# The four taps of the short convolution: accumulated in PSUM in two halves of 512 tokens, or in SBUF over all 1024

## The chip, the cores and the metric

The kernel runs on one core of a Trainium2 chip. The metric is the device time of one execution in microseconds (us), as the median of several runs. A profiled execution of the kernel gives the trace that the rows below are read from. The engines are named as the profile names them: PE is the tensor engine (PEld its weight loads), DVE the vector engine, ACT the scalar engine, POOL the GpSimd engine, and SP the engine that issues the DMAs. Each engine works through its own instructions strictly in the order in which they stand.

## What is computed

One layer of a hybrid decoder block on 1024 tokens with 1024 channels. A layer norm is followed by one input projection, whose columns go to two branches: a Mamba-2 (SSD) branch and a conformer convolution branch. Cut to what matters here:

```python
h = layer_norm(x, ln_emb_g, ln_emb_b)
proj = einsum('bld,de->ble', h, w_in)
xs, z, bm, cm, dt_raw, glu, cgate = split(proj)

xbc = concat([xs, bm, cm])                       # 1536 channels
xbc = silu(causal_depthwise_conv(xbc, ssm_conv_w, ssm_conv_b))   # 4 taps
...                                              # chunked scan, gate by silu(z), norm

u = glu[..., :1024] * sigmoid(glu[..., 1024:])
u = causal_depthwise_conv(u, conf_conv_w, conf_conv_b)           # 31 taps
u = silu(layer_norm(u)) * silu(cgate)
...
out = concat([y_ssm, u]) @ w_out + b_out         # then norm, per-layer gate, norm
```

The change is in the convolution with four taps, over the 1536 channels of `xbc`.

## The kernel before

Channels lie on the 128 partitions and tokens along the free dimension, so a tile is 128 channels by 1024 tokens, all in 32 bits. The input projection makes 44 such column tiles. For each one, `weights` loads the raw weights, ACT rounds them (`wh`, L119) and POOL takes the rest (`wl`, L120); `inproj` then runs 24 matmuls of 512 columns for each half of the tokens into one PSUM bank `ps` (L123 to L125), and ACT copies the bank out. There are three such banks, used in turn, so PE can run at most three halves ahead of ACT.

The tiles come in a fixed order. In each of eight rounds `conf_tile` makes the two tiles of a gated unit (`ga` L262, `tb` L265, multiplied into `u` at L279) and a convolution of 31 taps: six of the eight on DVE, which accumulates in a PSUM pair `pc` of 1024 columns (L291), and two (rounds 1 and 5) as products on ACT (`prod`, L285) that POOL adds up (`acc`, L286). Two other tiles follow in each round. Twelve of those are `xbc_tile`, the place of the change: ACT copies both halves into `xin` (L373), ACT makes the first tap (`cacc`, L247), DVE adds three more (L377), ACT applies the Silu (L378), and a DMA stores the tile. Others are `dt_path` (small DVE operations, L336 to L351), `decays`, and `z_tile` (L383). After the last round come `cs` (a sum on POOL, L630), `conf_norm` (its first matmul is `mu`, L390), the first `prep` (its transposes are `xtok`, L461, into the same PSUM pair as `pc`), and then the scan by chunks, the output projection and the gates.

A scheduler orders the instructions of each engine from its own estimates of time; the code sets what depends on what. PSUM has eight banks, all given out: three to `ps`, two to a tag `o` that serves small jobs in turn, one to a tag `b`, and two to the pair.

Of the kernel before, what the change touches and what calls it, by code (L numbers as in the profile page):

```python
# [11 lines left out]
ALU = mybir.AluOpType  # L12
# [13 lines left out]

# columns of the per-channel vectors
VEC = {}
# [18 lines left out]
def tile_block(ctx: ExitStack, tc: tile.TileContext, x, pT, wple, win, wdt, wout, wgate, vec, rows, heads, out):  # L47
# [17 lines left out]

# [1 line left out]
    BUFS = {"gt": 4, "xd": 2, "u": 2, "ha": 3, "y": 2, "xb": 2, "st": 1}  # L67
# [19 lines left out]

# [1 line left out]
    vc = const.tile([P, NVEC], F32, name="vc")  # L89
# [13 lines left out]
    nc.gpsimd.memset(mhalf, -0.5)  # L103
    # [s, l]: 1 where l >= s
    tri = const.tile([P, P], F32, name="tri")
    nc.gpsimd.affine_select(out=tri, in_=ones, pattern=[[1, P]], compare_op=ALU.is_ge, fill=0.0, base=0, channel_multiplier=-1)
    # adds rows h, 16 + h and 32 + h
    fold = const.tile([P, HEADS], F32, name="fold")
# [8 lines left out]
    def split(src, h, l, leng):  # L117
        """h: src rounded to the tensor engine's 12 bits; l: what is left, exactly."""
        nc.scalar.copy(out=h.bitcast(F32R), in_=src)  # L119
        leng.tensor_tensor(out=l.bitcast(F32R), in0=src, in1=h, op=ALU.subtract)  # L120
# [16 lines left out]
    def moments(src, tag):  # L137
        """mean and rstd of the rows of src [P, 1024]."""
        st = wk.tile([P, 2, 6], F32, name="st" + tag, tag="st" + tag)
        for i in range(2):  # L140
            nc.vector.bn_stats(out=st[:, i, :], in_=src[:, i * 512:(i + 1) * 512])
        mv = small("mv" + tag, 2)
        nc.vector.bn_aggr(out=mv, in_=st)
        return mv[:, 0:1], rstd_of(mv[:, 1:2], 1, tag, nc.gpsimd)
# [6 lines left out]

# [1 line left out]
    xts = [regB.tile([P, D], F32, name="xt", tag="B1") for t in range(NT)]  # L153
# [26 lines left out]

# [1 line left out]
    def weights(ct):  # L182
# [17 lines left out]
    def residual():  # L200
        ag, abb, bob = (work(n, "ha") for n in ("ag", "abb", "bob"))
        for i, tl in enumerate((ag, abb, bob)):
            nc.sync.dma_start(out=tl, in_=rows[i:i + 1, :].broadcast_to([P, D]))
        nc.gpsimd.tensor_scalar(out=ag, in0=ag, scalar1=ALPHA, scalar2=0.0, op0=ALU.mult, op1=ALU.add)
        nc.gpsimd.tensor_scalar(out=abb, in0=abb, scalar1=ALPHA, scalar2=0.0, op0=ALU.mult, op1=ALU.add)
        nc.gpsimd.tensor_tensor(out=abb, in0=abb, in1=bob, op=ALU.add)
        # alpha * h + b_out, by tokens
        for t in range(NT):
            nc.gpsimd.tensor_tensor(out=xts[t], in0=xts[t], in1=ag, op=ALU.mult)
            nc.gpsimd.tensor_tensor(out=xts[t], in0=xts[t], in1=abb, op=ALU.add)  # L210
            nc.sync.dma_start(out=ha_d[t], in_=xts[t])

    def ple_all():
        """the projected per-layer input, by tokens."""
        parts = {}
        tags = iter(["u", "u", "xd", "xd", "gt", "gt", "ha", "ha"])
        for src, nm in ((wple, "wp"), (pT, "pp")):
            for k in range(2):
                raw = work(nm + "raw", "xb") if nm == "wp" else regB.tile([P, L], F32, name=nm + "raw", tag="B2")
                parts[nm, k] = (raw, work(nm + "H", next(tags)), work(nm + "L", next(tags)))  # L220
        for half in range(2):
            hs = slice(half * 512, half * 512 + 512)
            for k in range(2):
                for src, nm in ((wple, "wp"), (pT, "pp")):
                    nc.sync.dma_start(out=parts[nm, k][0][:, hs], in_=src[:, k, hs])
                    split(*(a[:, hs] for a in parts[nm, k]), nc.vector)
        embed_load(0)
        nc.sync.dma_start(out=vc, in_=vec)
        nc.vector.tensor_scalar(out=hb, in0=v("bglu", 0, 16), scalar1=0.5, scalar2=None, op0=ALU.mult)
        parts = {i: (a[1].bitcast(F32R), a[2].bitcast(F32R)) for i, a in parts.items()}  # L230
        for t in range(NT):
            tk = slice(t * P, (t + 1) * P)
            pl = work("pl", "xb" if t % 4 > 1 else "y", L)
            for n in range(2):
                nn = slice(n * 512, n * 512 + 512)
                ps = bank("psp")
                for k in range(2):
                    three(ps, parts["pp", k][0][:, tk], parts["pp", k][1][:, tk], parts["wp", k][0][:, nn], parts["wp", k][1][:, nn], k == 0, k == 1)
                if (t + n) % 2:
                    nc.vector.tensor_copy(out=pl[:, nn], in_=ps)  # L240
                else:
                    nc.scalar.copy(out=pl[:, nn], in_=ps)
            nc.sync.dma_start(out=ple_d[t], in_=pl)
# [10 lines left out]
    def conf_tile(j):  # L254
        """GLU and the causal convolution of 128 channels."""
        ga = work("ga", "gt")
# [44 lines left out]
    def dt_path():  # L301
# [7 lines left out]
        nc.sync.dma_start(out=hd, in_=heads.unsqueeze(0).broadcast_to([P, 2, HEADS]))  # L309
        # both parts of the weights side by side  # L310
        nc.scalar.copy(out=wh2[:, :, 0:HEADS].bitcast(F32R), in_=raw)
# [22 lines left out]

        # softplus(v) = max(v, 0) + 2 atanh(e / (2 + e)), e = exp(-|v|)
        nc.vector.tensor_tensor(out=b3(vv), in0=b3(pst[:, 0:P]), in1=bh(hd[:, 0, :]), op=ALU.add)  # L336
# [16 lines left out]
    def decays():  # L353
        """dec holds dt * a at first: its sums over the tokens of each chunk, and what follows from them."""
        ar, er = (wk.tile([P, P], F32, name=n, tag="dg") for n in ("ar", "er"))
# [14 lines left out]
    def xbc_tile(ct, i):  # L370
        xin = work("xin", "xb", 3 + L)
        nc.gpsimd.memset(xin[:, 0:3], 0.0)
        inproj(ct, lambda hs, ps: nc.scalar.copy(out=xin[:, 3 + hs.start:3 + hs.stop], in_=ps))  # L373
        acc = work("cacc", "ha")
        first_tap(FT4, acc, xin[:, 0:L], v("scw", i * 4), v("scb", i))
        for j in range(1, 4):
            nc.vector.scalar_tensor_tensor(out=acc, in0=xin[:, j:j + L], scalar=v("scw", i * 4 + j), in1=acc, op0=ALU.mult, op1=ALU.add)  # L377
        nc.scalar.activation(out=acc, in_=acc, func=AF.Silu)  # L378
        nc.sync.dma_start(out=xbc_d[:, :, i, :].rearrange("t p l -> p t l"), in_=by_chunk(acc))
# [36 lines left out]
    def out_weight(src, get, tag, last, scale=None, leng=nc.gpsimd):  # L416
        """last: a place for the raw one, where those that share the tag leave none."""
        raw = work("wor", last) if last else get("wor", tag)
# [8 lines left out]

# [1 line left out]
    state = work("state", "st")  # L429
# [8 lines left out]
    def prep(c):  # L438
        """what chunk c needs besides the state: decays times C.B, x * dt, B by tokens."""
        xb = slabs(work("xb", "xb", 12 * P), 12)  # L440
# [8 lines left out]
        for q in range(2):  # L449
            er = ea_d[c * HEADS:(c + 1) * HEADS, :].rearrange("(t q) l -> q t l", q=2)[q]  # L450
            nc.sync.dma_start(out=ea[q * HD:(q + 1) * HD], in_=er.unsqueeze(0).broadcast_to([HD, NK, P]))
        # exp(acs[l] - acs[s]); the part l < s is held at exp(0) here and dropped with C.B
        for h in range(HEADS):
# [30 lines left out]
    def chunk(c, sz, xb, gg, ea, xdt, xdd, btok):  # L484
        y = slabs(work("y", "y"))
        for g in range(2):
            # from the state, scaled by exp(acs[l])
            ys = y[:, g * 4:g * 4 + 4, :]
# [34 lines left out]
    def mean_square(c, y, ea):  # L523
        """rstd of the two groups of channels of the gated output."""
        sq = ea.rearrange("p (g t) l -> p g t l", g=2)
# [21 lines left out]
    def conf_out(c, mH, mL, ha):  # L547
        """conformer half of the output projection"""
        for n in range(2):
# [14 lines left out]
    def affine(o, src, mu, rs, g, b):  # L564
        """(src - mu) * rs * g + b"""
        nc.vector.scalar_tensor_tensor(out=o, in0=src, scalar=mu, in1=g, op0=ALU.subtract, op1=ALU.mult)
        nc.vector.scalar_tensor_tensor(out=o, in0=o, scalar=rs, in1=b, op0=ALU.mult, op1=ALU.add)

    def out_proj(c, yH, yL):
        """the SSM half of the output projection, and the norm"""  # L570
        r = work("r", "ha")
# [21 lines left out]
    def gate(c, r, hTH, hTL):  # L593
        """the per-layer input, gated, and the norm"""
        pl = work("pl3", "st")
# [75 lines left out]

# [1 line left out]
    ready, last = out_proj(0, *ys.pop(0)), None  # L673
# [58 lines left out]
```

## Time and profile before

| What | Value |
|---|---|
| Time, median of 3 runs | 932.74 us (928.87 to 934.99) |
| Span of the profiled execution | 927.1 us |
| PE busy | 877.1 us, 95% of the span |
| DVE busy | 708.6 us, 76% |
| POOL busy | 534.4 us, 58% |
| ACT busy | 364.8 us, 39% |
| Mean granted clock of PE | 0.985 of full speed |

The span runs from the first to the last instruction of the profiled execution; the timed runs stand 1.8 to 7.9 us above it. Busy shares are means over stages with different limits, so they say little about any one stage.

### The profile page before, as it was taken

To read this page: it belongs to the slowest core of one execution; us is meant where nothing else is said; L and a number is where in the kernel's file an instruction comes from. 1 tells how busy PE (TensorE), PEld (TensorE's weight loads), DVE (VectorE), ACT (ScalarE), POOL (GpSimd) and SP (SyncE) were. 2 spreads that over 40 slices of the span, in tenths; PEclk is the share of its full clock that TensorE was granted. 3 is DMA by queue.
4 is the path that set the end of the run, shared out by engine and by line. 5 is a ranking of instruction groups with operands and counts; after the bars stand their busy time and mean duration, and the time that the engine had idled before them with its cause. 6 is when DMAs were issued, how large, how long until landed. Compare 5 with 4: busy or idle time off the path is not lost.

```text
span 927.1 us, 10959 instructions
## 1 busy us (share of the span) xinstructions
PE 877.1 (95%) x4141; PEld 711.0 (77%) x4141; DVE 708.6 (76%) x830; ACT 364.8 (39%) x513; POOL 534.4 (58%) x298
## 2 busy tenths in 40 slices
PE   6989998989999999999899999999999889999996
PEld 5857787868787888788688887777777668888885
DVE  7868997498999989989626523998885786666665
ACT  3532244665423435555446533644343421111001
POOL 2559836999924249999792254676757442222211
PEclk9999999989999999999999999999999999999999
DMA  9703241321213121322322388888887902222111
GB/s 337 264 24 107 77 157 46 96 69 46 78 37 113 52 86 53 123 97 80 114 100 83 103 304 271 300 273 230 283 264 261 353 25 92 91 90 91 69 46 68
DMA packets 67716, 126.42 MB, mean 136 GB/s; under 512 B 4176, under 2 KB 41552, under 8 KB 67664
## 3 DMA queue, kind: packets, MB, share of 16 engines
q1 hardware_dynamic: 67664, 125.73, 40.4%
q8 instruction: 32, 0.52, 0.2%
q14 instruction: 20, 0.16, 0.1%
HBM read 89.93 MB, written 35.78 MB: 136 GB/s over the span
## 4 chain that ended last, share of the span: by engine, by line
PE 47%; DVE 20%; POOL 13%; DMA 11%; issue 6%; ACT 3%; SPq 1%; POOLq 0%; DVEq 0%; ACTq 0%
POOL acc L286 8%; DVE pc L291 7%; PE ps L123 6%; PE ps L124 6%; PE ps L125 6%; DVE cacc L377 4%; PE psg L123 3%; PE psg L125 3%; PE psg L124 3%; DMA wor<-in_wout_dram 3%; PE pss L123 3%; PE pss L125 3%; PE pss L124 3%; DMA xb<-xbc_d 2%; POOL wl L120 2%
## 5 line engine op out<-in xcount | busy, mean ns | idle before, releaser
L123 PE MATMUL ps<-hH,wl 128*128 128x512 f32 x704 | 278.4, 397 | 12.7 <-ACT ga L262 6.2
L124 PE MATMUL ps<-hL,wh 128*128 128x512 f32 x704 | 278.0, 395 | 1.0 <-DVE hL L179 1.0
L125 PE MATMUL ps<-hH,wh 128*128 128x512 f32 x704 | 278.1, 395 | 0.0
L291 DVE SCALAR_TENSOR_TENSOR pc<-u,vc,pc 128x1024 f32<-128x1024 f32 x174 | 223.8, 1286 | 4.5
L123 PEld LDWEIGHTS ps<-hH,wl 128*128 128x128 f32 x704 | 133.9, 191 | 44.7 <-issue 7.7
L286 POOL TENSOR_TENSOR acc<-acc,prod 128x1024 f32<-128x1024 f32 x60 | 160.2, 2671 | 13.3 <-ACT acc L282 9.3
L124 PEld LDWEIGHTS ps<-hL,wh 128*128 128x128 f32 x704 | 134.2, 191 | 29.3 <-DVE hL L179 1.5
L125 PEld LDWEIGHTS ps<-hH,wh 128*128 128x128 f32 x704 | 134.2, 191 | 28.4 <-issue 0.2
L120 POOL TENSOR_TENSOR wl<-wraw,wh 128x1024 fp32r<-128x1024 f32 x44 | 110.6, 2513 | 53.2 <-ACT wh L119 23.0
L132 POOL TENSOR_SCALAR ve<-mv 128x1 f32<-128x1 f32 x24 | 21.7, 907 | 121.3 <-DVE mv L611 88.4
L285 ACT ACTIVATE prod<-u,vc 128x1024 f32<-128x1024 f32 x60 | 68.8, 1150 | 51.4 <-POOL acc L286 44.9
L377 DVE SCALAR_TENSOR_TENSOR cacc<-xin,vc,cacc 128x1024 f32<-128x1024 f32 x36 | 76.9, 2135 | 7.4 <-ACT cacc L247 4.7
L119 ACT CAST wh<-wraw 128x1024 fp32r<-128x1024 f32 x44 | 46.2, 1051 | 82.6 <-DMA wraw<-in_win_dram 47.8
L455 DVE TENSOR_SCALAR gt<-gt,acs 128x128 f32<-128x128 f32 x128 | 42.0, 397 | 25.4 <-POOL qs L398 17.3
L123 PE MATMUL psg<-woh,hTL 128*128 128x512 f32 (+1 forms) x136 | 52.9, 389 | 4.8 <-DVE hTL L120 4.8
L123 PE MATMUL pso<-woh,mL 128*128 128x512 f32 x128 | 51.6, 406 | 2.8 <-POOL mL L120 1.8
L123 PE MATMUL pss<-woh,yL 128*128 128x512 f32 x128 | 50.8, 397 | 3.4 <-DVE r L580 3.4
L120 POOL TENSOR_TENSOR wol<-wor,woh 128x1024 fp32r<-128x1024 f32 x12 | 32.7, 2743 | 36.1 <-ACT woh L119 36.1
L125 PE MATMUL pso<-woh,mH 128*128 128x512 f32 x128 | 53.2, 417 | 0.0
L125 PE MATMUL psg<-woh,hTH 128*128 128x512 f32 (+1 forms) x136 | 52.6, 387 | 0.0
L124 PE MATMUL psg<-wol,hTH 128*128 128x512 f32 (+1 forms) x136 | 52.1, 383 | 0.0
L124 PE MATMUL pso<-wol,mH 128*128 128x512 f32 x128 | 50.9, 397 | 0.0
(184 smaller groups left out, 1435.5 us busy)
## 6 DMA issues: line engine op xcount, KB each, us to landing
wraw<-in_win_dram SPq DMA_DIRECT2D x44, 512.0 KB, 4.1
gt<-acs_d SPq DMA_DIRECT2D x16, 512.0 KB, 4.6
wor<-in_wout_dram SPq DMA_DIRECT2D x16, 512.0 KB, 6.1
xbc_d<-cacc SPq DMA_DIRECT2D x12, 512.0 KB, 3.4
xb<-xbc_d SPq DMA_DIRECT2D x8, 768.0 KB, 6.3
xt<-in_x_dram SPq DMA_DIRECT2D x8, 512.0 KB, 9.2
ple_d<-pl SPq DMA_DIRECT2D x8, 512.0 KB, 5.0
ha_d<-xt SPq DMA_DIRECT2D x8, 512.0 KB, 5.2
```

Source lines behind the costliest of these rows:

```text
L119: nc.scalar.copy(out=h.bitcast(F32R), in_=src)
L120: leng.tensor_tensor(out=l.bitcast(F32R), in0=src, in1=h, op=ALU.subtract)
L123: mm(ps, lhsT=ll, rhs=rh, start=first, stop=False)
L124: mm(ps, lhsT=lh, rhs=rl, start=False, stop=False)
L125: mm(ps, lhsT=lh, rhs=rh, start=False, stop=last)
L132: eng.tensor_scalar(out=ve, in0=var, scalar1=EPS, scalar2=None, op0=ALU.add)
L285: nc.scalar.activation(out=pr, in_=u[:, i:i + L], func=AF.Copy, scale=v("ccw", j * KC + i))
L286: nc.gpsimd.tensor_tensor(out=acc, in0=acc, in1=pr, op=ALU.add)
L291: nc.vector.scalar_tensor_tensor(out=pc if i + 1 < KC else acc, in0=u[:, i:i + L], scalar=v("ccw", j * KC + i), in1=pc, op0=ALU.mult, op1= ...
L377: nc.vector.scalar_tensor_tensor(out=acc, in0=xin[:, j:j + L], scalar=v("scw", i * 4 + j), in1=acc, op0=ALU.mult, op1=ALU.add)
L455: nc.vector.tensor_scalar(out=sl, in0=sl, scalar1=col(acs, c, h), scalar2=0.0, op0=ALU.subtract, op1=ALU.min)
```

## The change

The taps are now made for 512 tokens at a time, in one PSUM bank of the tag `o` (two banks, in turn): ACT writes the first tap of a half into the bank, DVE adds three taps in the bank, and ACT applies the Silu from the bank into the same half of `cacc` in SBUF. The store to HBM stays one DMA for the whole tile. The diff also takes out comments and docstrings elsewhere, which changes no instruction.

```diff
     def xbc_tile(ct, i):
...
         acc = work("cacc", "ha")
-        first_tap(FT4, acc, xin[:, 0:L], v("scw", i * 4), v("scb", i))
-        for j in range(1, 4):
-            nc.vector.scalar_tensor_tensor(out=acc, in0=xin[:, j:j + L], scalar=v("scw", i * 4 + j), in1=acc, op0=ALU.mult, op1=ALU.add)
-        nc.scalar.activation(out=acc, in_=acc, func=AF.Silu)
+        for half in range(2):
+            o = half * 512
+            pc = obank("pc4")
+            first_tap(FT4, pc, xin[:, o:o + 512], v("scw", i * 4), v("scb", i))
+            for j in range(1, 4):
+                nc.vector.scalar_tensor_tensor(out=pc, in0=xin[:, o + j:o + j + 512], scalar=v("scw", i * 4 + j), in1=pc, op0=ALU.mult, op1=ALU.add)
+            nc.scalar.activation(out=acc[:, o:o + 512], in_=pc, func=AF.Silu)
         nc.sync.dma_start(out=xbc_d[:, :, i, :].rearrange("t p l -> p t l"), in_=by_chunk(acc))
```

In the changed kernel the taps on DVE stand at L380 and the Silu at L381. The scheduler's order moves with them. The matmuls of the projection keep their order; three places where other rows moved:

DVE, the taps of the first `xbc_tile` beside the first 31-tap convolution (`pc` at L291) and the small operations of `dt_path` (`dt`), before:

```order
L340 RECIPROCAL dt_748<-dt_748 128x128
L291 SCALAR_TENSOR_TENSOR pc<-u,vc,pc 128x1024
L341 TENSOR_TENSOR dt_748<-dt_748 128x128
L377 SCALAR_TENSOR_TENSOR cacc<-xin,vc,cacc 128x1024
L291 SCALAR_TENSOR_TENSOR pc<-u,vc,pc 128x1024
L342 TENSOR_TENSOR dt_748<-dt_748 128x128
L377 SCALAR_TENSOR_TENSOR cacc<-xin,vc,cacc 128x1024
L291 SCALAR_TENSOR_TENSOR pc<-u,vc,pc 128x1024
L343 TENSOR_SCALAR dt_748<-dt_748 128x128
L377 SCALAR_TENSOR_TENSOR cacc<-xin,vc,cacc 128x1024
```

The same place now (`pc_886` and `pc_892` are the banks of the two halves):

```order
L380 SCALAR_TENSOR_TENSOR pc_886<-xin,vc,pc_886 128x512
L336 TENSOR_TENSOR dt_748<-pstd,dt_749 128x128
L291 SCALAR_TENSOR_TENSOR pc<-u,vc,pc 128x1024
L380 SCALAR_TENSOR_TENSOR pc_886<-xin,vc,pc_886 128x512
L337 SCALAR_TENSOR_TENSOR dt_748<-dt_748 128x128
L291 SCALAR_TENSOR_TENSOR pc<-u,vc,pc 128x1024
L380 SCALAR_TENSOR_TENSOR pc_886<-xin,vc,pc_886 128x512
L339 TENSOR_SCALAR dt_748<-dt_748 128x128
L291 SCALAR_TENSOR_TENSOR pc<-u,vc,pc 128x1024
L340 RECIPROCAL dt_748<-dt_748 128x128
L380 SCALAR_TENSOR_TENSOR pc_892<-xin,vc,pc_892 128x512
```

Three rows of 1024 became six of 512 (the last two stand below these rows). They begin after the fifth of `pc`'s operations (L249 and four taps) instead of after the ninth, and still stand one at a time between taps of the long convolution.

ACT, the second and third `xbc_tile`, beside the start of the convolution of round 1 (`acc`, `prod`), before:

```order
L373 COPY xin<-ps_1114 128x512
L373 COPY xin<-ps_1140 128x512
L247 ACTIVATE cacc<-xin,vc 128x1024
L119 CAST wh<-wraw 128x1024
L282 ACTIVATE acc<-u,vc 128x1024
L373 COPY xin<-ps_1181 128x512
L285 ACTIVATE prod<-u,vc 128x1024
L378 ACTIVATE cacc<-cacc 128x1024
L285 ACTIVATE prod<-u,vc 128x1024
L373 COPY xin<-ps_1207 128x512
```

And now:

```order
L247 ACTIVATE pc_1174<-xin,vc 128x512
L373 COPY xin<-ps_1147 128x512
L247 ACTIVATE pc_1180<-xin,vc 128x512
L381 ACTIVATE cacc<-pc_1174 128x512
L119 CAST wh<-wraw 128x1024
L282 ACTIVATE acc<-u,vc 128x1024
L373 COPY xin<-ps_1195 128x512
L247 ACTIVATE pc_1248<-xin,vc 128x512
L381 ACTIVATE cacc<-pc_1180 128x512
L285 ACTIVATE prod<-u,vc 128x1024
L381 ACTIVATE cacc<-pc_1248 128x512
L373 COPY xin<-ps_1221 128x512
```

Each half has a Silu of its own, and three Silus now stand ahead of the last copy, `xin` of the third tile's second half (`ps_1207` before, `ps_1221` now), where one stood before.

PE, the place of the transposes `xtok` among the matmuls of a `z_tile`, before:

```order
L124 MATMUL ps_3344<-hL_135,wh 128x512
L125 MATMUL ps_3344<-hH_127,wh 128x512
L123 MATMUL ps_3344<-hH_128,wl 128x512
L124 MATMUL ps_3344<-hL_136,wh 128x512
L125 MATMUL ps_3344<-hH_128,wh 128x512
L123 MATMUL ps_3344<-hH_129,wl 128x512
L124 MATMUL ps_3344<-hL_137,wh 128x512
L461 MATMUL xtok<-ident,xb 128x128 x8
```

And now (`ps_3428` is the bank of the same half):

```order
L125 MATMUL ps_3402<-hH_131,wh 128x512
L123 MATMUL ps_3402<-hH_132,wl 128x512
L124 MATMUL ps_3402<-hL_140,wh 128x512
L125 MATMUL ps_3402<-hH_132,wh 128x512
L464 MATMUL xtok<-ident,xb 128x128 x8
L123 MATMUL ps_3428<-hH_125,wl 128x512
```

The transposes moved up by 14 matmuls, to the start of that half; `mu` moved up by six in the same way.

## Rows read from the trace of the kernel before

**Rows 1.** Windows, PE alone: window, its length, PE busy (instructions), granted clock, DMA.

```profile
57.00:460.00 403.00, 388.43 (x1675) 0.97 0.26 84
460.00:565.00 105.00, 105.00 (x480) 1.00 0.43 146
113.80:117.20 3.40, 3.40 (x10) 0.50 1.02 381
199.10:205.90 6.80, 5.24 (x12) 0.50 0.72 231
```

**Rows 2.** Waits of PE from 60 to 460 us: total, times, longest.

```profile
PE ps L123 <- ACT ga L262: 6.2, 4, 3.5
PE ps L123 <- ACT xin L373: 3.7, 3, 2.6
PE xtok L461 <- DVE acc L291: 2.0, 1, 2.0
PE ps L123 <- ACT tb L265: 1.1, 2, 0.6
PE mu L390 <- POOL cs L630: 0.6, 1, 0.6
```

**Rows 3.** Timeline of PE: start, duration, instruction, [idle before, and who ended it].

```profile
113.40 0.47 PE L123 MATMUL ps<-hH,wl 128*128 128x512 f32 x1 [1.95 <-ACT ga L262]
...
151.03 0.48 PE L123 MATMUL ps<-hH,wl 128*128 128x512 f32 x1 [2.60 <-ACT xin L373]
...
200.66 0.76 PE L123 MATMUL ps<-hH,wl 128*128 128x512 f32 x1 [3.47 <-ACT ga L262]
...
447.47 0.77 PE L461 MATMUL xtok<-ident,xb 128*128 128x128 f32 x5 [1.96 <-DVE acc L291]
```

**Rows 4.** Timeline of ACT just ahead of the first two of those.

```profile
110.68 1.06 ACT L378 ACTIVATE cacc<-cacc 128x1024 f32<-128x1024 f32 x1 [13.51 <-DVE cacc L377]
...
148.32 1.06 ACT L378 ACTIVATE cacc<-cacc 128x1024 f32<-128x1024 f32 x1 [8.66 <-DVE cacc L377]
```

**Rows 5.** Groups on DVE, first 311 to 332 us, then 354 to 380 us.

```profile
L377 DVE SCALAR_TENSOR_TENSOR cacc<-xin,vc,cacc 128x1024 f32<-128x1024 f32 x6 | 7.7, 1278 | 0.0
...
L377 DVE SCALAR_TENSOR_TENSOR cacc<-xin,vc,cacc 128x1024 f32<-128x1024 f32 x6 | 14.2, 2360 | 0.3 <-ACT cacc L247 0.2
```

**Rows 6.** Groups on POOL, first 354 to 380 us, then 380 to 440 us.

```profile
L286 POOL TENSOR_TENSOR acc<-acc,prod 128x1024 f32<-128x1024 f32 x7 | 22.1, 3157 | 0.4
...
L286 POOL TENSOR_TENSOR acc<-acc,prod 128x1024 f32<-128x1024 f32 x19 | 46.6, 2455 | 1.0
```

**Rows 7.** Groups by form, whole span: busy us, mean ns | idle before, releasers.

```profile
L291 DVE SCALAR_TENSOR_TENSOR pc<-u,vc,pc 128x1024 f32<-128x1024 f32 x174 | 223.8, 1286 | 4.5
L286 POOL TENSOR_TENSOR acc<-acc,prod 128x1024 f32<-128x1024 f32 x60 | 160.2, 2671 | 13.3 <-ACT acc L282 9.3 <-ACT prod L285 1.2
L377 DVE SCALAR_TENSOR_TENSOR cacc<-xin,vc,cacc 128x1024 f32<-128x1024 f32 x36 | 76.9, 2135 | 7.4 <-ACT cacc L247 4.7 <-POOL wl L120 2.6
L285 ACT ACTIVATE prod<-u,vc 128x1024 f32<-128x1024 f32 x60 | 68.8, 1150 | 51.4 <-POOL acc L286 44.9 <-DVE u L279 6.5
L580 DVE SCALAR_TENSOR_TENSOR r<-pss,rsm,r 128x512 f32<-128x512 f32 x32 | 23.8, 747 | 10.2 <-PE pss L125 10.0
L247 ACT ACTIVATE cacc<-xin,vc 128x1024 f32<-128x1024 f32 x12 | 14.9, 1240 | 0.3
L378 ACT ACTIVATE cacc<-cacc 128x1024 f32<-128x1024 f32 x12 | 12.7, 1061 | 68.8 <-DVE cacc L377 68.8
L262 ACT ACTIVATE ga<-ps,hb 128x512 f32<-128x512 f32 x16 | 10.9, 678 | 6.2 <-PE ps L125 6.2
L383 ACT ACTIVATE zt<-ps 128x512 f32<-128x512 f32 x16 | 9.2, 584 | 1.0 <-PE ps L125 1.0
```

**Rows 8.** Timeline of ACT, then of DVE: the last `tb` and its product `u`.

```profile
391.59 0.67 ACT L265 ACTIVATE tb<-ps,hb 128x512 f32<-128x512 f32 x1
...
401.05 2.72 DVE L279 SCALAR_TENSOR_TENSOR u<-tb,ga 128x1024 f32<-128x1024 f32 x1
```

## The prediction

> **What bounds the kernel now.** I read the windows first, for PE alone. From 460 to 565 us PE is busy for all of the 105 us at full clock; from 57 to 460 us, the stage in which the change lies, it is busy for 388 of 403 us at 0.97 [rows 1]. So PE's own matmuls set this stage, and a gain can come only from what PE loses there. The waits of PE come next: 6.2 + 3.7 + 2.0 + 1.1 + 0.6 = 13.6 us [rows 2]. Almost all are for ACT to empty a bank `ps`. The timeline says where: three waits of 1.95, 2.60 and 3.47 us for ACT, at 113, 151 and 201 us, and one of 1.96 us for the last tap of the last long convolution on DVE, at 447 us [rows 3]; six smaller ones make up 3.0 us and the wait for `mu` 0.6 us. Each of the four long waits is followed or accompanied by a stretch at the lower clock, 0.50 of 2.4 GHz, that is the level of 1.2 GHz: 3.4 us of it behind the first, 6.8 us around the third [rows 1], and 3.4 us again behind the second and the fourth. Each time PE had just stood idle for about 2 us. A stretch of 3.4 us at half speed costs 1.7 us; of the 6.8 us PE worked 5.24, so 2.6 us. Together 3 x 1.7 + 2.6 = 7.7 us. **PE loses 13.6 + 7.7 = 21.3 us in this stage; that is about the most that the change can bring.**
>
> Why was ACT late? Its own timeline, just ahead of the first two waits, shows a Silu of `cacc` that stood idle for 13.51 and 8.66 us until DVE had made the last tap [rows 4]. ACT takes its instructions in order, so the copies that empty the banks stood behind that Silu. All such waits together are 68.8 us, the largest of ACT; the next, 44.9 us, is products `prod` waiting for POOL's adds [rows 7].
>
> Why are the taps slow? In a stretch in which POOL adds nothing up, a tap takes 1278 ns; in one in which POOL runs the other long convolution, 2360 ns [rows 5]. POOL pays as well: its adds take 3157 ns beside those taps and 2455 ns after them [rows 6]. The taps of the long convolution, which accumulate in PSUM and read only one tensor from SBUF, take 1286 ns on the mean of 174, many of which run beside POOL's two convolutions [rows 7]. So the cost goes with taps that have both tensors in SBUF, and each side holds up the other.
>
> **The change part by part.** *DVE.* Removed: 36 taps of 2135 ns, 76.9 us [rows 7]. Added: 72 taps of 512 columns with one operand and the result in PSUM. No row shows this. From below: half of an L291 tap, 643 ns, with no fixed part counted twice. From above: L580, 747 ns, an operation of the same kind on 512 columns that reads PSUM and SBUF [rows 7]. I take 700 ns, between the two: 72 x 0.70 = 50.4 us (46 to 54). DVE is relieved of **26.5 us** (23 to 31). Where POOL is quiet the new form is no gain: 36 x 1.278 = 46.0 us for the old [rows 5].
>
> The Trainium skill (Advanced Engine Details and Errata, The Read-Write Bubble) speaks against this edit: it counts a latency between instructions that large tiles spread, and says that the vector engine lies closer to SBUF than to PSUM. The trace agrees with the first in kind: 50.4 against 46.0 us where POOL is quiet. It doesn't bear out the second, with 1286 ns in PSUM beside 1278 ns in SBUF. By that rule alone DVE would get some 4 us longer; the rows beside POOL outweigh it.
>
> *POOL.* Sixty adds of 2671 ns on the mean [rows 7]; at 2455 ns they would save 60 x 0.216 = **13 us**, spread over the two convolutions of rounds 1 and 5.
>
> *ACT.* Removed: 12 first taps of 1240 ns and 12 Silus of 1061 ns, 27.6 us. Added: 24 first taps of 512 columns, for which L262 stands (the same function, 678 ns), and 24 Silus read from PSUM, for which L383 stands (584 ns): 30.3 us [rows 7]. The 2.7 us more are hidden by ACT's idle time. What counts is where ACT waits, below.
>
> *PE, SP.* No matmul and no DMA is added; the order of the projection's matmuls is the same, and on SP a few neighbouring transfers change places.
>
> *What becomes of each loss of PE.*
> First wait (113 us): the taps of the first tile begin four long taps sooner (4 x 1.29 = 5.1 us) and take six times 0.70 instead of three times 2.1 or more, 2 us less. The copy of `ga` comes about 7 us sooner, and 1.95 us were missing. Gone, with its slow stretch: 1.95 + 1.7 = 3.65 us.
> Second (151 us): here too four long taps stand ahead of the next tile's first tap instead of eight, and the tile's taps are 2 us shorter; again some 7 us against 2.60 us missing. Three Silus now stand ahead of that copy instead of one. DVE makes the taps for the first two between long taps, at 3 x (0.70 + 1.29) = 6.0 us a half, and for the third in a row, 2.1 us; the margin shrinks and, I think, holds. 2.60 + 1.7 = 4.3 us.
> Third (201 us): ACT is behind because its products wait for POOL. Six adds before 200 us lie beside a tap in the timeline; 6 x 0.70 us [rows 6] = 4.2 us against 3.47 us missing. Close, but POOL also starts its sum sooner, since it waits for ACT's first products. 3.47 + 2.6 = 6.1 us.
> Small ones: half of 3.0 us, 1.5 us. I don't see which fall.
> Fourth (447 us): the last long convolution begins on DVE at 401 us with no idle time before, 9 us after ACT had its `tb` ready [rows 8]: DVE is late by its own queue. With the 15.6 us above, `tb` is ready at 392.3 - 15.6 = 376.7 us and DVE free at about 401 - 26.5 = 374.5 us. The last tap ends some 24 us sooner, at 423 us; PE comes to `xtok` at 445.5 - 15.6 - 3.1 (14 matmuls of about 0.22 us) = 426.8 us. Gone: 1.96 + 1.7 = 3.66 us.
> Sum: 3.65 + 4.3 + 6.1 + 1.5 + 3.66 = 19.2 us. I take off 2 us for a wait that 24 Silus in place of 12 will surely bring somewhere. **Gain 17 us**, from a span of 927.1 to 910 us. The median of the runs is 5.6 us above the span, and that stays: 932.7 - 17 = **916 us**.
>
> *What comes after 460 us.* `mu` needs POOL's sum of the last round-5 add. POOL starts that convolution when PE has delivered its input, so it shifts with PE and is shorter by about half of the 13 us; the 0.6 us of waiting for `mu` may grow a little. From there the chain goes on through work that starts from `mu` and from the end of the projection, and I expect it to move as a whole.
>
> **The rivals.**
> *New Silu waits take the place of the old.* A half's taps take 6.0 us between long taps, while PE fills a bank in 24 x 0.22 = 5.3 us (105 us for 480 matmuls [rows 1]). If ACT now waits at every half, PE's lead of three banks is eaten. For it: 68.8 us of waiting, with DVE still nearly full. Against it: the copies now stand between the Silus, each wait is half as long, and the two that cost PE time before were 13.51 and 8.66 us long. It would keep half of the first three losses: gain 17 - 7 - 2 = 8 us or less, 925 to 929 us.
> *The part after 460 us doesn't follow,* because loads there are paced by their own queue. For it: it moves much more data than the first. Against it: its loads go into places that the projection and `mu`'s results set free. Half the gain would be left, 924 us, or none, 933 us.
> *DVE waits for ACT's first taps: slower.* Each of the 24 halves now needs a first tap from ACT, which stands there behind products that wait for POOL, and on DVE all the taps of the long convolution stand behind it. At one add of POOL for each half, 24 x 2.46 = 59 us, DVE loses 59 - 26.5 = 32 us; the last convolution, `xtok` and `mu` come that much later, while the first three losses of PE (14 us) are still saved: 18 us slower, 951 us. It turns at 26.5 / 24 = 1.1 us a half. For it: 44.9 us of such waits over 60 products. That is 0.75 us each, and only the halves in rounds 1 and 5 meet any.
> *The new tap is no cheaper beside POOL than the old.* Then DVE gains nothing and only the order changes: 930 to 936 us. Against it stand the 174 taps of L291.
>
> **How the numbers follow.** Forecast (909 to 922 us): 0.63. New Silu waits: 0.19. The rest doesn't follow: 0.09. DVE waits for ACT: 0.06. No cheaper tap: 0.03. The bottom of the range is the whole 21.3 us and 3 us of scatter between runs, 908 us; the top takes in the second rival's and most of the first one's cases, 930 us. One per cent, about what a measurement of this kernel can tell from no change, is 9.3 us. Below 923.4 us lie the forecast and a third of the first two rivals, 0.72; above 942 us lies the slower one, 0.06; the rest is 0.22.
>
> **What would show it.** In the changed profile the taps should take 0.65 to 0.75 us with or without POOL, POOL's adds 2.4 us throughout, the Silu waits of ACT well under 68.8 us with none above 8 us. PE's waits for ACT from 60 to 460 us should fall from 11 to under 4 us, with no stretch at half clock at 113, 151 and 201 us, and `mu` should come some 17 us sooner. The prediction is wrong if PE waits for ACT as long as before at other places, if DVE idles for `pc4`, or if `mu` comes sooner and the end doesn't.

## The result and the profile after

The changed kernel takes 905.61 us (median of 4 runs, 904.01 to 912.1) against 932.43 us (median of 4, 928.87 to 934.99) for the kernel before: a ratio of 0.972, with a 95% interval of 0.969 to 0.976. That is 26.8 us faster. The forecast was 916 us in a range of 908 to 930: the sign was right, and the gain was larger than the range allowed for. The profiled execution has a span of 902.3 us (927.1 before), so 24.8 us are to be found in the trace. The other 2 us lie in how the runs scatter: the median of these four stood 5.3 us above the span before, and stands 3.3 us above it now. The two profiled executions were themselves timed at 928.87 and 904.01 us, each the fastest of its four.

The windows for PE alone answer to [rows 1] (window, its length, PE busy with its instructions, granted clock, DMA).

```profile
57.00:460.00 403.00, 401.06 (x1784) 1.00 0.28 89
440.00:545.00 105.00, 105.00 (x500) 1.00 0.49 157
```

From 57 to 460 us PE is busy for 401.06 us instead of 388.43, at full clock throughout instead of 0.97. The second row is about the stretch that lay at 460 to 565 us before: it was full then and is full now. The waits of PE from 57 to 460 us answer to [rows 2] (total, times, longest):

```profile
PE ps L124 <- DVE hL L179: 1.0, 1, 1.0
PE ps L123 <- DVE hH L177: 0.9, 1, 0.9
```

Both stand at the start of the stage, between 57 and 61 us. No wait for ACT is left, none for `xtok`, none for `mu`. The page's chain of waits, by engine, shows what this makes of the kernel; PE held 47% of it before, DVE 20%, POOL 13% and the DMA 11%:

```profile
PE 80%; DVE 9%; DMA 5%; issue 2%; POOL 2%; ACT 1%; SPq 0%; POOLq 0%; DVEq 0%; ACTq 0%
```

The groups by form answer to [rows 7] (busy us, mean ns | idle before, releasers). The last row belongs to an experiment below.

```profile
L291 DVE SCALAR_TENSOR_TENSOR pc<-u,vc,pc 128x1024 f32<-128x1024 f32 x174 | 223.9, 1287 | 3.5
L286 POOL TENSOR_TENSOR acc<-acc,prod 128x1024 f32<-128x1024 f32 x60 | 145.3, 2422 | 17.6 <-ACT acc L282 14.7
...
L380 DVE SCALAR_TENSOR_TENSOR pc<-xin,vc,pc 128x512 f32<-128x512 f32 x72 | 53.7, 750 | 6.3 <-ACT pc L247 3.8 <-POOL acc L286 2.3
L247 ACT ACTIVATE pc<-xin,vc 128x512 f32<-128x512 f32 x24 | 18.8, 782 | 0.7
L381 ACT ACTIVATE cacc<-pc 128x512 f32<-128x512 f32 x24 | 14.2, 590 | 36.0 <-DVE pc L380 35.9
...
L479 DVE TENSOR_TENSOR gt<-gt,cbm 128x1024 f32<-128x1024 f32 x16 | 28.9, 1841 | 1.2 <-ACT gt L460 1.1
```

The taps cost DVE 53.7 us instead of 76.9, and the taps of the long convolution, which were in PSUM already, cost what they did. POOL's adds fell from 2671 to 2422 ns, 14.9 us in all. The Silus wait for DVE for 35.9 us instead of 68.8. The timeline of ACT shows them at the place where the second loss of PE began before (start, duration, [idle before]):

```profile
132.95 0.60 ACT L381 ACTIVATE cacc<-pc 128x512 f32<-128x512 f32 x1 [6.56 <-DVE pc L380]
...
138.50 0.60 ACT L381 ACTIVATE cacc<-pc 128x512 f32<-128x512 f32 x1 [1.58 <-DVE pc L380]
```

The longest wait of a Silu is now 6.56 us; in [rows 4] it was 13.51 us. Where the time was won is read from PE's timeline in both kernels. First the kernel before, with five rows that are used further down:

```profile
111.07 0.39 PE L125 MATMUL ps<-hH,wh 128*128 128x512 f32 x1
...
163.60 0.39 PE L357 MATMUL psa<-dec,tri 128*128 128x128 f32 x2
...
235.43 0.39 PE L124 MATMUL ps<-hL,wh 128*128 128x512 f32 x1
235.65 0.39 PE L125 MATMUL ps<-hH,wh 128*128 128x512 f32 x1
236.88 0.47 PE L123 MATMUL ps<-hH,wl 128*128 128x512 f32 x1 [0.84 <-ACT xin L373]
237.19 0.39 PE L124 MATMUL ps<-hL,wh 128*128 128x512 f32 x1
...
454.64 1.98 PE L390 MATMUL mu<-cs,invd 128*128 128x512 f32 x4 [0.58 <-POOL cs L630]
...
567.61 1.97 PE L501 MATMUL yd<-gt,xdt 128*64 128x128 f32 x32
```

Then the changed one:

```profile
154.80 0.39 PE L357 MATMUL psa<-dec,tri 128*128 128x128 f32 x2
...
422.67 1.03 PE L464 MATMUL xtok<-ident,xb 128*128 128x128 f32 x8
...
429.23 1.88 PE L393 MATMUL mu<-cs,invd 128*128 128x512 f32 x4
...
543.44 1.97 PE L504 MATMUL yd<-gt,xdt 128*64 128x128 f32 x32
```

`psa` comes 8.8 us sooner: that is the first two waits. `mu` comes 25.4 us sooner, of which about 1.4 us are a place in PE's order that lies some matmuls earlier. The first `yd` after the projection comes 24.2 us sooner, and the end of the span 24.8. So nearly all of it was won by 430 us, and what follows moved as a whole. The length of the stage says the same: from the matmul of `ps` that starts at 63.4 us in both kernels to the same one shortly behind `mu` (at 456.7 us before, 432.6 us now) it was 393.3 us and is 369.2 us.

### The profile page after: what moved, and what is told of

Read it like the earlier page. It is cut to its first block, busy times and chain, and to the rows that moved or that the text cites. A ratio compares the mean times of both kernels' runs of the same rounds, so it can differ in the third digit from the quotient of the medians.

```text
span 902.3 us, 11019 instructions
## 1 busy us (share of the span) xinstructions
PE 866.1 (96%) x4141; PEld 705.9 (78%) x4141; DVE 681.9 (76%) x866; ACT 372.0 (41%) x537; POOL 518.3 (57%) x298
## 4 chain that ended last, share of the span: by engine, by line
PE 80%; DVE 9%; DMA 5%; issue 2%; POOL 2%; ACT 1%; SPq 0%; POOLq 0%; DVEq 0%; ACTq 0%
PE ps L124 17%; PE ps L125 17%; PE ps L123 17%; PE psg L123 3%; PE psg L125 3%; PE psg L124 3%; PE pss L123 3%; PE pss L125 3%; PE pss L124 3%; PE pso L123 2%; PE pso L124 2%; PE pso L125 2%; DMA wor<-in_wout_dram 1%; DMA yraw<-y_d 1%; DVE gt L458 1%
## 5 line engine op out<-in xcount | busy, mean ns | idle before, releaser
L123 PE MATMUL ps<-hH,wl 128*128 128x512 f32 x704 | 274.2, 391 | 2.8 <-DVE hH L177 2.8
L124 PE MATMUL ps<-hL,wh 128*128 128x512 f32 x704 | 274.6, 391 | 1.0 <-DVE hL L179 1.0
L125 PE MATMUL ps<-hH,wh 128*128 128x512 f32 x704 | 274.2, 390 | 0.0
L291 DVE SCALAR_TENSOR_TENSOR pc<-u,vc,pc 128x1024 f32<-128x1024 f32 x174 | 223.9, 1287 | 3.5
L286 POOL TENSOR_TENSOR acc<-acc,prod 128x1024 f32<-128x1024 f32 x60 | 145.3, 2422 | 17.6 <-ACT acc L282 14.7
L123 PEld LDWEIGHTS ps<-hH,wl 128*128 128x128 f32 x704 | 131.8, 188 | 30.1 <-DVE hH L177 3.2
L124 PEld LDWEIGHTS ps<-hL,wh 128*128 128x128 f32 x704 | 132.2, 188 | 29.0 <-DVE hL L179 1.5
L125 PEld LDWEIGHTS ps<-hH,wh 128*128 128x128 f32 x704 | 132.2, 188 | 27.5 <-issue 0.2
L458 DVE TENSOR_SCALAR gt<-gt,acs 128x128 f32<-128x128 f32 x128 | 45.1, 423 | 24.4 <-DMA gt<-acs_d 24.3
L380 DVE SCALAR_TENSOR_TENSOR pc<-xin,vc,pc 128x512 f32<-128x512 f32 x72 | 53.7, 750 | 6.3 <-ACT pc L247 3.8
L125 PE MATMUL pss<-woh,yH 128*128 128x512 f32 x128 | 50.5, 395 | 0.0
```

Source lines behind the costliest of these rows:

```text
L123: mm(ps, lhsT=ll, rhs=rh, start=first, stop=False)
L124: mm(ps, lhsT=lh, rhs=rl, start=False, stop=False)
L125: mm(ps, lhsT=lh, rhs=rh, start=False, stop=last)
L286: nc.gpsimd.tensor_tensor(out=acc, in0=acc, in1=pr, op=ALU.add)
L291: nc.vector.scalar_tensor_tensor(out=pc if i + 1 < KC else acc, in0=u[:, i:i + L], scalar=v("ccw", j * KC + i), in1=pc, op0=ALU.mult, op1= ...
L380: nc.vector.scalar_tensor_tensor(out=pc, in0=xin[:, o + j:o + j + 512], scalar=v("scw", i * 4 + j), in1=pc, op0=ALU.mult, op1=ALU.add)
```

## The experiments

**The theory:** a tap with both tensors in SBUF waits for POOL and holds POOL up; ACT's Silu, and behind it the copies that empty the banks `ps`, are late by that; PE idles and then runs at half clock. **The rivals:** the gain comes from the halves and the new order on ACT alone; or from DVE's smaller total load; or from POOL's faster adds. Each time below is a median, beside that of the kernel before in the same set of runs.

**1. The halves without PSUM.** Everything is as in the changed kernel, but the taps accumulate in SBUF.

```diff
-            pc = obank("pc4")
+            pc = acc[:, o:o + 512]
```

> The two halves of the changed kernel with their taps accumulated in SBUF, as before; ACT's order stays nearly that of the changed kernel. Theory (the gain comes from taps that no longer meet POOL at SBUF): a half tap takes 0.7 us where POOL is quiet and about 1.5 to 2 us where it runs, DVE's taps 100 us in all, POOL's adds over 2.6 us on the mean; PE waits for ACT for 10 us or more again; 928 to 945 us. Rival (the gain comes from the halves and the order that the scheduler made of them): 905 to 912 us, taps of 0.7 us.

It took 944.88 us beside 930.88, a ratio of 1.015 (1.011 to 1.018). Its groups by form and its waits of PE from 60 to 460 us:

```profile
L380 DVE SCALAR_TENSOR_TENSOR cacc<-xin,vc,cacc 128x512 f32<-128x512 f32 x72 | 96.9, 1351 | 3.8 <-ACT cacc L247 3.5 <-issue 0.2
...
L286 POOL TENSOR_TENSOR acc<-acc,prod 128x1024 f32<-128x1024 f32 x60 | 152.5, 2541 | 23.4 <-ACT acc L282 15.7 <-ACT prod L285 5.2
```

```profile
PE ps L123 <- ACT xin L373: 10.4, 5, 5.5
PE ps L123 <- ACT ga L262: 6.7, 3, 2.8
```

With the same halves, the same ACT instructions and nearly their order, PE waits for ACT longer than before. So halves by themselves, in SBUF, bring nothing: they cost 14 us. Whole taps in PSUM were not tried, so whether the halves matter there is not shown. Half a tap takes 1351 ns, far more than half of the whole one's 2135. POOL's adds came to 2541 ns, a little under the 2.6 us expected.

**2. One half in PSUM, the other in SBUF.**

```diff
-            pc = obank("pc4")
+            pc = acc[:, o:o + 512] if half else obank("pc4")
```

> Only the first half's taps are in PSUM, the second half's in SBUF. Theory: about half of the taps meet POOL, half of PE's waits come back, 912 to 928 us. Rival (halves and order): 905 to 912 us.

It took 922.47 us beside 930.88, 0.991 (0.987 to 0.994). Its groups by form hold both kinds of tap side by side:

```profile
L380 DVE SCALAR_TENSOR_TENSOR cacc<-xin,vc,cacc 128x512 f32<-128x512 f32 x36 | 50.5, 1402 | 3.0 <-ACT cacc L247 2.9
L380 DVE SCALAR_TENSOR_TENSOR pc<-xin,vc,pc 128x512 f32<-128x512 f32 x36 | 27.0, 749 | 0.6 <-ACT pc L247 0.6
```

In one execution, next to the same kind of work on POOL, the tap in SBUF takes 1402 ns and the one in PSUM 749. The time lies between experiment 1 and the changed kernel, as the theory has it. POOL's adds take 2469 ns here, so 12.1 of the 14.9 us that they lose in the changed kernel are gone already; and still PE waits for ACT (60 to 460 us):

```profile
PE ps L123 <- ACT xin L373: 4.6, 4, 2.1
PE ps L123 <- ACT ga L262: 3.5, 3, 1.7
```

So faster adds on POOL are not the whole of the gain.

**3. The kernel before, with POOL's adds cut to 128 of 1024 columns.** This leaves out most of the sums of rounds 1 and 5.

```diff
-                nc.gpsimd.tensor_tensor(out=acc, in0=acc, in1=pr, op=ALU.add)
+                nc.gpsimd.tensor_tensor(out=acc[:, 0:P], in0=acc[:, 0:P], in1=pr[:, 0:P], op=ALU.add)
```

> The kernel before, with POOL's adds of its two long convolutions cut to 128 of 1024 columns (most of those sums is left out). Theory: the taps in SBUF take 1.28 us in rounds 1 and 5 too, PE's waits at 151 and 201 us and the small ones go, the wait at 113 us stays, since there POOL works on the residual; 908 to 918 us. Rival (long Silu waits come from whole tiles of taps, not from POOL): the taps stay above 2 us and the wait at 151 us stays; 925 us or more.

It took 919.4 us beside 930.88, 0.987 (0.983 to 0.992): less gain than expected. The timeline of PE still holds the first two waits:

```profile
113.24 0.47 PE L123 MATMUL ps<-hH,wl 128*128 128x512 f32 x1 [1.90 <-ACT ga L262]
...
151.29 0.76 PE L123 MATMUL ps<-hH,wl 128*128 128x512 f32 x1 [3.07 <-ACT xin L373]
```

The wait at 201 us and the later ones for ACT are gone. So those belong to the stretches in which taps and POOL's adds run side by side, as I had said. This run makes both shorter (the taps take 1586 ns on the mean instead of 2135), so it doesn't part the one from the other. The one at 151 us, which I expected to go as well, doesn't. A new thought was needed for it: that it is still the first tile's delay, carried on along DVE's queue. The first tile's taps lie beside other work of POOL, the adds of the residual (L210), which this edit leaves alone. Experiments 9 and 10 try this.

**4. One more tap in each half of the changed kernel** (the fourth tap is added twice).

```diff
-            for j in range(1, 4):
+            for j in (1, 2, 3, 3):
```

> The changed kernel with a fourth tap per half on DVE (the last one twice, so the sum is another): 24 operations of 0.75 us more, DVE's taps 72 us in all, nearly the 76.9 us of before, but in PSUM. Theory: what counts is how late the taps come behind POOL, so most of the gain stays, 904 to 912 us. Rival (the gain is DVE's lighter load as such): 918 to 930 us.

It took 916.26 us beside 930.88 (911.65 to 923.39), 0.985 (0.978 to 0.992): slower than expected. Of its groups by form the taps; from its timeline of PE, and from its windows for PE alone, the two places of the loss:

```profile
L380 DVE SCALAR_TENSOR_TENSOR pc<-xin,vc,pc 128x512 f32<-128x512 f32 x96 | 70.2, 749 | 2.3 <-POOL acc L286 1.2 <-ACT pc L247 0.7
```

```profile
483.91 0.71 PE L412 MATMUL rb<-dg,ones 128*128 128x128 f32 x4 [2.96 <-DVE dg L411]
```

```profile
564.70:578.40 13.70, 9.38 (x50) 0.50 0.49 138
```

The stage up to 460 us has no wait of PE for ACT, `xtok` or `mu`, though DVE spends 70.2 us on these taps, nearly the 76.9 us of before. So it isn't the total of DVE's load that cost PE time there. The loss comes afterwards: a wait for `dg`, a small tensor that DVE makes for a later step, at 484 us, and 13.7 us at half clock from 565 us. Whether DVE's load brought it there, or the instructions' changed order, this run doesn't tell.

**5. Experiment 1 with the short adds of experiment 3** (both edits, as above).

> The halves in SBUF and POOL's adds cut to 128 columns (most of those two sums is left out). Tells what the order of the halves does when POOL is quiet in rounds 1 and 5. Theory: the wait at 151 us, which stayed with short adds and whole tiles, is a matter of the place of the taps in DVE's order and goes; the wait at 113 us, where POOL works on the residual, stays in part; 908 to 916 us. Rival (PSUM is needed there too): the wait at 151 us stays, 918 to 925 us.

It took 911.32 us beside 929.45, 0.981 (0.978 to 0.983). The tap in SBUF falls from 1351 to 974 ns, and the ratio from 1.015 to 0.981: the cost of a tap in SBUF hangs on POOL. The wait at 151 us went only in part: at the same matmul, now at 148.06 us, PE stops for 1.41 us, and no longer for ACT but for POOL's `wl`. Others came earlier. The timeline of PE, then that of ACT:

```profile
129.02 0.50 PE L123 MATMUL ps<-hH,wl 128*128 128x512 f32 x1 [2.04 <-ACT xin L373]
...
148.06 0.47 PE L123 MATMUL ps<-hH,wl 128*128 128x512 f32 x1 [1.41 <-POOL wl L120]
```

```profile
125.36 2.19 ACT L285 ACTIVATE prod<-u,vc 128x1024 f32<-128x1024 f32 x2 [3.78 <-DVE u L279]
...
128.39 0.57 ACT L373 COPY xin<-ps 128x512 f32<-128x512 f32 x1
```

ACT's copy of a bank stands behind products that waited 3.78 us for DVE's `u`. DVE is late from the first tile on, where the adds of the residual are as long as ever.

**6. The changed kernel with the short adds.** The edit of experiment 3, with the taps in PSUM.

> The changed kernel with POOL's adds cut to 128 columns (most of those two sums is left out). Theory: with the taps in PSUM nothing is left for PE to wait for between 60 and 460 us, so relieving POOL brings nothing there; 898 to 910 us, xtok within 2 us of the changed kernel. Rival (POOL still delays the stage): xtok comes 4 us or more sooner.

It took 907.54 us beside 929.45, 0.977 (0.975 to 0.979), no better than the changed kernel. PE has no wait for ACT, `xtok` or `mu` in the stage, and `xtok` starts at 422.08 us instead of 422.67. With the taps in PSUM, cutting POOL's adds further brings the stage nothing. That doesn't make the 14.9 us that POOL won a by-product. Ahead of the third wait of the kernel before, ACT's timeline shows products that stood idle for POOL's adds, and a Silu that did not stand idle at all:

```profile
192.04 1.16 ACT L285 ACTIVATE prod<-u,vc 128x1024 f32<-128x1024 f32 x1 [1.70 <-POOL acc L286]
195.38 1.15 ACT L285 ACTIVATE prod<-u,vc 128x1024 f32<-128x1024 f32 x1 [2.19 <-POOL acc L286]
...
197.85 1.06 ACT L378 ACTIVATE cacc<-cacc 128x1024 f32<-128x1024 f32 x1
...
199.85 0.67 ACT L262 ACTIVATE ga<-ps,hb 128x512 f32<-128x512 f32 x1
```

So the third wait came to ACT by way of POOL, as the prediction has it, and not by way of a Silu. No run has the taps in PSUM and POOL's adds as slow as before, so how much of the gain went by POOL and how much by DVE stays open.

**7. The same idea for another operation:** the tanh of the gate goes into PSUM, and `u` is made from it by halves.

```diff
-            nc.scalar.activation(out=tb[:, hs], in_=ps, func=AF.Tanh, scale=0.5, bias=hb[:, 8 + j:9 + j])
+            tp = obank("tp")
+            nc.scalar.activation(out=tp, in_=ps, func=AF.Tanh, scale=0.5, bias=hb[:, 8 + j:9 + j])
+            nc.vector.scalar_tensor_tensor(out=u[:, KC - 1 + hs.start:KC - 1 + hs.stop], in0=tp, scalar=1.0, in1=ga[:, hs], op0=ALU.add, op1=ALU.mult)
...
-        nc.vector.scalar_tensor_tensor(out=u[:, KC - 1:], in0=tb, scalar=1.0, in1=ga, op0=ALU.add, op1=ALU.mult)
```

> The changed kernel, with the tanh of each gated unit put into a PSUM bank of the tag o and its product u made by halves from there: one more operation that no longer has both inputs in SBUF. Theory: the product costs DVE two times 0.75 us instead of 1.8 us and POOL loses fewer pauses, but PE waits for nothing in this stage, so the time stays, 900 to 912 us. Rival (DVE still sets the end): 3 us or more faster than the changed kernel, under 900 us.

It took 912.51 us beside 929.45, 0.982 (0.979 to 0.984): just above the 900 to 912 us expected, and worse than the changed kernel. A half of `u` takes 688 ns, as hoped, but PE waits anew (waits of PE, 60 to 460 us):

```profile
PE psr L364 <- DVE acs L359: 2.7, 1, 2.7
```

`acs` is what DVE copies out of `psa`, and PE's small matmul `psr` reads it. DVE's timeline shows where that copy stood:

```profile
165.53 0.69 DVE L266 SCALAR_TENSOR_TENSOR u<-tp,ga 128x512 f32<-128x512 f32 x1 [6.72 <-ACT tp L265]
...
168.91 0.28 DVE L359 COPY acs<-psa 128x128 f32<-128x128 f32 x1
```

`psa` was done at 161 us, but the copy stands behind the second half of `u`, which waited 6.72 us for ACT's tanh. In the changed kernel it stands ahead of `u` and starts at 155.45 us. PE idles until 169 us and runs at half clock for some 3.5 us behind it. So what the row shows is a place in DVE's order; that the shared banks `o` have a part in it is not shown.

**8. The same idea after the stage:** the masked product `cbm`, which DVE multiplies into `gt`, stays in the PSUM bank in which it was made.

```diff
-        cbm = wk.tile([P, 2, P], F32, name="cbm", tag="cbm", bufs=1)
-        nc.vector.tensor_tensor(out=cbm, in0=bps[:, 2 * P:4 * P].rearrange("p (g l) -> p g l", g=2),
-                                in1=tri.unsqueeze(1).broadcast_to([P, 2, P]), op=ALU.mult)
+        cbm = bps[:, 2 * P:4 * P].rearrange("p (g l) -> p g l", g=2)
+        nc.vector.tensor_tensor(out=cbm, in0=cbm, in1=tri.unsqueeze(1).broadcast_to([P, 2, P]), op=ALU.mult)
```

> The changed kernel with the masked products cbm left in their PSUM bank, so that the 16 products of the decays with them have one operand in PSUM. Theory: these fall from about 1.93 to 1.3 us and POOL's adds and splits of the chunk stage shorten; whether PE gains hangs on whether it waits for them (1.5 us in all by the trace): 898 to 908 us. Rival: the bank, which is the only one of its tag, is held longer and PE waits for it, 910 to 925 us.

It took 902.22 us beside 929.45, 0.971 (0.970 to 0.973). Of its groups by form, the row that answers to L479 above:

```profile
L478 DVE TENSOR_TENSOR gt<-gt,bps 128x1024 f32<-128x1024 f32 x16 | 18.8, 1211 | 1.2 <-ACT gt L460 1.1
```

1211 ns instead of 1841, 10 us of DVE over 16 products. Against the kernel before in its own set of runs the gain is 27.2 us, beside 26.8 us for the changed kernel in its set. Experiment 12 puts the two side by side.

**9. Only the first tile of the short convolution by halves in PSUM** (`i == 8`), the others as before.

```diff
-        for half in range(2):
-            o = half * 512
+        if i == 8:
+            for half in range(2):
...
+        else:
+            first_tap(FT4, acc, xin[:, 0:L], v("scw", i * 4), v("scb", i))
```

> Only the first tile (the one beside the residual on POOL) has its taps in PSUM by halves; the other eleven as before. Theory (the delay of the first tile's taps is carried along DVE's queue to the second wait): the waits at 113 and 151 us both go or shrink under 1 us, the later ones stay; psa 7 to 9 us sooner, 920 to 926 us. Rival (each tile's own taps make its own wait): only the wait at 113 us goes, psa 4 us sooner, 925 to 930 us.

It took 924.42 us beside 929.58, 0.995 (0.993 to 0.997). Its timeline of PE:

```profile
152.92 0.39 PE L357 MATMUL psa<-dec,tri 128*128 128x128 f32 x2
...
191.31 0.55 PE L123 MATMUL ps<-hH,wl 128*128 128x512 f32 x1 [3.50 <-ACT ga L262]
```

`psa` comes 10.7 us sooner than before. Of that 1.9 us are scatter: this execution was that much ahead already at 63 us, before the first of these taps. The other 8.8 us are what the changed kernel wins there too: the waits at 113 and 151 us are gone, although the second tile's taps are the old ones. DVE's timeline has the first of those, here and in the kernel before:

```profile
131.85 1.28 DVE L386 SCALAR_TENSOR_TENSOR cacc<-xin,vc,cacc 128x1024 f32<-128x1024 f32 x1
```

```profile
141.28 1.28 DVE L377 SCALAR_TENSOR_TENSOR cacc<-xin,vc,cacc 128x1024 f32<-128x1024 f32 x1
```

It is no shorter, but it starts 9.4 us sooner. The wait at 201 us stays, at 191 now, and so do most of the later ones. This is what the carried delay says.

**10. All but the first tile in PSUM** (`i != 8` in the place of `i == 8`).

> The other way round: the first tile's taps whole and in SBUF, the other eleven by halves in PSUM. Theory (carried delay): the wait at 113 us stays, one of 1 us or more stays between 125 and 155 us, all later ones go; 909 to 914 us. Rival (own taps): only the wait at 113 us stays, psa 4 to 5 us sooner than before, 907 to 911 us.

It took 913.52 us beside 929.58, 0.984 (0.980 to 0.987). Its timeline of PE, then those of DVE and of POOL around the first tile's taps:

```profile
113.40 0.47 PE L123 MATMUL ps<-hH,wl 128*128 128x512 f32 x1 [1.90 <-ACT ga L262]
...
131.81 0.50 PE L123 MATMUL ps<-hH,wl 128*128 128x512 f32 x1 [1.84 <-ACT xin L373]
```

```profile
95.79 3.41 DVE L386 SCALAR_TENSOR_TENSOR cacc<-xin,vc,cacc 128x1024 f32<-128x1024 f32 x1
...
107.21 3.43 DVE L386 SCALAR_TENSOR_TENSOR cacc<-xin,vc,cacc 128x1024 f32<-128x1024 f32 x1
```

```profile
90.96 16.24 POOL L210 TENSOR_TENSOR xt<-xt,abb 128x1024 f32<-128x1024 f32 x6
107.16 2.40 POOL L120 TENSOR_TENSOR wl<-wraw,wh 128x1024 fp32r<-128x1024 f32 x1
```

The wait at 113 us stays, a second one follows at 132 us, and of the later ones 0.26 us are left. Behind the first of the two the granted clock stays at 1.00 (113.8 to 117.2 us), where the kernel before fell to 0.50 after nearly the same wait; behind the second it falls to 0.50. So not every wait of this length brings a slow stretch. The three taps take 3.41 us and more each, the first two beside POOL's six adds of 2.71 us, the third beside `wl`. In the changed kernel a tap takes 0.75 us there.

**11 and 12. The changed kernel once more, and experiment 8 once more,** beside the same runs of the kernel before, which are also those of 9 and 10.

> The changed kernel once more, beside the next. Theory: 903 to 908 us, no wait of PE for ACT between 60 and 460 us, xtok at 422 to 424 us. Rival (part of its gain was chance of one profile): such waits show up, xtok after 426 us.

> The kernel with cbm left in PSUM once more, on the same chip as the changed one. Theory: DVE's products stay at 1.21 us and it is 2 to 5 us faster than the changed kernel, 899 to 904 us. Rival: no difference, within 1.5 us of it.

The changed kernel took 904.51 us beside 929.58, 0.973 (0.971 to 0.975); experiment 8 took 901.17, 0.970 (0.968 to 0.972). So `cbm` in PSUM is worth 3.3 us side by side; the intervals overlap slightly, and that it is faster than the changed kernel is likely rather than certain. In the changed kernel `xtok` comes at 420.4 us, sooner than the 422 to 424 us expected: this execution was 2.3 us ahead at its start, and its stage is 369.2 us long again. By the medians the first tile alone is worth 5.2 us (experiment 9 against the kernel before) to 9.0 us (experiment 10 against the changed one) of the changed kernel's 25.1. The same stage in the traces, 385.4 us in experiment 9 and 375.8 in experiment 10, gives 7.9 and 6.6 us of 24.1.

## Why the prediction was right in sign and too small

The chain of causes stood in the main, apart from the cause of the second wait, and the part after 460 us moved as a whole. What was off are sizes, all on one side. To size the terms I set the starts of the same matmul of `ps`, counted in PE's order, in both traces beside each other, from one wait's place to the next.

| loss of PE | forecast, us | measured, us |
|---|---|---|
| first wait, 113 us | 3.65 | 3.8 |
| second, 151 us | 4.3 | 5.0 |
| third, 201 us | 6.1 | 6.3 |
| small ones, 230 to 385 us | 1.5 | 4.3 |
| fourth, 447 us, with `mu` | 3.66 | 4.7 |
| new waits for Silus | -2 | 0 |
| sum | 17 | 24.1 |

- **The step that failed is the ceiling,** "about the most that the change can bring" with 21.3 us. It was summed from the idle times of PE's rows, and these undercount a wait. A matmul of `ps` is recorded as 0.39 us long, but the next one starts 0.23 us after it. At 237 us the rows of before go from 235.65 to 236.88: 1.23 us from start to start, so 1.00 us lost where the row says 0.84; and the matmul behind the wait takes 0.31 us to the next start instead of 0.23. That is 0.24 us for each wait and 2.4 us for ten. At 111.07 us it is the same, 2.33 - 0.23 = 2.10 us against 1.95 [rows 3]. With it the ceiling is 23.7 us, against 24.1 measured. The bottom of the range stood on that ceiling; with 23.7 us it would have been 906 us, and what is left to 905.61 us is within the scatter of the runs.
- **The small waits** were taken at half; all went, with their undercounted part. No row gave a reason for the half. The table's last row of them holds five of the six; the one at 132 us, about 0.5 us, is in the row of the second wait.
- **The 2 us taken off for new Silu waits** fell away. The Silus still wait for 35.9 us, but never so that a bank `ps` is missing; this rival, with 0.19, fell. The largest gap between the sum and the result comes from the last two terms, 2.8 + 2 us.
- **The taps:** 750 ns, the upper of my two bounds, where I took 700. DVE is relieved of 76.9 - 53.7 = 23.2 us instead of 26.5. It made no difference to the stage, as experiment 4 shows with 16.5 us more of it. Where POOL is quiet the new taps cost 54 us (72 of 752 ns) against the 46.0 us of the old form, where the forecast had 50.4.
- **POOL:** 14.9 us instead of 13, with adds of 2422 ns throughout. Experiment 6 shows that nothing in the stage hangs on a further cut.
- **ACT:** 18.8 + 14.2 = 33.0 us where 30.3 was forecast, since a first tap takes 782 ns and not L262's 678. It stayed hidden.
- **The second wait** was forecast in size, but its cause only in part. I put it down to the second tile's own taps and the long taps ahead of them. Experiment 9 removes it without touching that tile, and experiment 3 leaves it in place although it shortens the work beside that tile. It was the first tile's delay, carried on. That the size fitted was in part luck.
- **The third wait** and most of the later ones came from taps beside POOL's adds: experiment 3, which shortens those adds, and experiment 10, which puts those taps into PSUM, both remove them. The third came by the path that the prediction names, products held up by POOL.
- **The other rivals fell too.** DVE idles for ACT's first taps for 3.8 us in 24 halves, 0.16 us each, where the slower case needed 1.1. That the new tap is no cheaper beside POOL is excluded by experiment 2, with 749 beside 1402 ns.
- **The offset** of the median above the span, taken as 5.6 us, came out at 3.3 us. That and the 0.7 us gained after the stage are the rest of the 10.4 us between forecast and result: 7.1 + 2.3 + 0.7, and 0.3 of rounding.

Left open: how the gain divides between DVE and POOL, what brought the losses behind the stage in experiment 4, and whether another order on DVE would have saved experiment 7.

## What to carry to other kernels

Look for operations of DVE with two tensors in SBUF that run beside POOL, compare their time with a stretch in which POOL is quiet, and put one operand into PSUM where a bank is free. Count what a wait of PE costs from start to start, with the half-clock stretch where one follows, and don't discount small waits of the same cause. And where engines work in order, ask of each wait whether its cause lies one tile earlier: the first delayed tile here cost 5 to 9 us by itself.

## What the runs showed of the hardware that was not expected

- A tap of two tensors in SBUF doesn't get cheaper by halves. In experiment 1 the 72 half taps cost 96.9 us, the 36 whole ones before 76.9. Over the undisturbed time (1278 ns a whole tap [rows 5], 747 ns a half one from 318 to 323 us in experiment 1) that is 0.86 us more for each whole tap and 0.60 us for each half one, where half of 0.86 would be 0.43. Of the taps that ran while POOL worked on a large tile, the whole ones (23 of 36) took 1.34 us more each and the half ones (37 of 72) 1.18 us. So halving a tap saves little of its wait for POOL. The Trainium skill (SBUF — State Buffer, Who interferes with whom) says that an instruction of DVE with two inputs in SBUF contends with one of POOL that reads SBUF, and that one with a single input there doesn't. The traces agree: 1402 and 749 ns side by side in experiment 2.
- How much it costs depends on what POOL runs: 3.41 us a tap beside the adds of the residual, 2.36 us beside the long convolution [rows 5].
- ACT's first tap takes 782 ns into PSUM, and 814 ns into SBUF in experiment 1's group by form: a small gain there as well. DVE's half tap, where POOL is quiet, takes 752 ns in PSUM (286 to 306 us of the changed kernel) beside the 747 ns in SBUF, so for DVE the gain lies in not meeting POOL.
